# Four of eight query tiles on float16 parts, and one bfloat16 load where two float32 loads stood

## The chip, the cores and the metric

The kernel runs on one core of a Trainium2 chip. The metric is the device time of one launch, in microseconds (us); lower is better. The core has a matrix engine (TensorE, in the profile PE, with its weight loads as PEld), a vector engine (VectorE, DVE), a scalar engine (ScalarE, ACT), GpSimd (POOL) and SyncE (SP). DMA transfers are issued from queues, here almost all from those of SP and POOL. Operands lie in SBUF, 128 partitions wide; matrix products accumulate in eight PSUM banks.

## The reference

Two layers of a small diffusion transformer, on 256 tokens of x and 256 tokens of context, 2048 wide, in float32. Layer 0 is a Fourier branch, layer 1 an attention branch with a sink:

```python
def _fourier_branch(h, w_in, w_mix):
    u, z = jnp.split(h @ w_in, 2, axis=-1)
    f = jnp.fft.fft2(ug, axes=(1, 3), norm='ortho').real        # ug: u in 16 groups of 256
    f = jnp.einsum('bngc,gcd->bngd', f, w_mix)
    return f * jax.nn.silu(z)

# layer 1, x tokens (the context gives keys and values alone):
q, k, v, z = jnp.split(h @ w_in, [D_BRANCH, D_BRANCH + kvw, D_BRANCH + 2 * kvw], axis=-1)
q, k = _axial_rope(q, rows, cols), _axial_rope(k, rows, cols)
o = softmax over [scores of a band of 128 and of the context, sink]
y = o * jax.nn.silu(z)

# around each layer:
h = _rmsnorm(x, norm_g[i]) * (1 + scale) + shift                 # shift, scale, gate from c @ ada_w
x = x + gate * (y @ w_out[i])
```

Query, key and value come out of one weight matrix; the 4096 query columns are cut into eight tiles of 512 (eight heads of 64 each).

## The kernel before

**Precision.** A float32 product is made of three matmuls (`mm3`, lines 145 to 147): each operand is cut into a high and a low part, and high by high, high by low and low by high are summed in PSUM. There are two kinds of parts. `half_split` makes two float32r tiles of 128x1024: a cast on ACT (L66, `wh`) and a subtraction on DVE (L67, `wl`). `split16` makes one tile with two float16 halves (`wf`): a scaled copy on ACT (L137) and a multiply-and-subtract on DVE (L138); it needs a power of two `up` that brings the weights into float16's range, which is worked out from the sum of the squares of the weights. A pair of float32r tiles takes two of the six slots of the pool `ws`, a float16 pair one.

**Stages**, with their place in the profiled span:

1. 0 to 365 us: the Fourier branch's u part.
2. 365 to 658: the gate product z of layer 0, in blocks of 48 matmuls, on float16 parts; its weights `wz` come on SP's queue, 1 MiB a block, and are squared on ACT (L81) for their own scale. Beside it the adaptation products run on DVE (L792, `zr` and `wa` from `in_adw`), and the weights of later float16 products are read ahead, only to be squared and summed: `scan_loads` issues from POOL (L836) two loads of 128x512 float32 per step, `scan_sums` squares each on ACT (L829) with a running sum into a column of `scn`.
3. 658 to 996: the out product of layer 0 in two sweeps of 16 steps, float16; the same kind of reading ahead for the key and value weights and part of layer 1's out weights (`scan_loads1`, L821).
4. 996 to 1085: keys and values, float16. The normalised input of layer 1 is made as float16 pairs `hz` (16 tiles, both token groups) and, in `make_hx1`, for the x tokens as float32r parts `hx1`.
5. 1085 to 1543: attention. An order of units is written out by hand: query tile n+1 (eight units of 12 matmuls of 128x512) and four blocks of layer 1's gate z1 (two units of 24 matmuls of 128x256 each) stand beside the four attention blocks of tile n. All q and z1 units here are float32r: the weights are cut by `half_split` one unit ahead (`prep`), and the stationary operand of q is `hx1`. An attention block makes scores (L1499), the mask and row maximum on DVE (L1502), the exponential on ACT (L1506), the normalised probabilities on DVE (L1522) and ACT (L1521), a transposing DMA, and the product with v (L1533). `finish_q` makes the row scales and the rotary positions of a query tile.
6. 1543 to 1735: the out product of layer 1 and the last norm.

What sets the order is the program as written, with `issue_after` edges, and a scheduler that lays each engine's instructions in one queue. Weights stand in three raw tiles of 1 MiB, and the activations, the tiles read ahead among them, in a pool of 33 slots of 2 KB per partition.

Of the kernel before, what the change touches and what calls it, by code (L numbers as in the profile page):

```python
# [17 lines left out]
P = 128  # L18
# [4 lines left out]
N = 256  # L23
# [9 lines left out]
def tile_dit(ctx: ExitStack, tc: tile.TileContext, a: dict, out: bass.AP):  # L33
# [776 lines left out]
    ek, upk, dnk, kw = (keepc[:, c : c + 1] for c in range(4))  # L810
    gsz, shz = adab[:, 0, 1], adab[:, 0, 2]
    yq = adab[:, 1, 0].rearrange("p k s -> p (k s)")
    wst = [a["wkv"][i] for i in range(8)] + [a["wo1b"][i] for i in range(12)] + [a["wo1c"][i] for i in range(6)]
    scans1 = iter(range(52))

    def scan_loads1(n):
        for j in [next(scans1) for _ in range(n)]:
            for q in range(2):
                t = act()
                c = (j % 2 * 2 + q) * 512  # L820
                nc.gpsimd.dma_start(t, wst[j // 2][:, c : c + 512])  # L821
                c = j * 2 + q
                c += 80 if c < 28 else -28
                pend.append((t, scn[:, c : c + 1]))

    def scan_sums():
        while pend:
# [2 lines left out]

    def scan_loads(n):
        for j in [next(scans) for _ in range(n)]:
            for q in range(2):
                t = act()
                c = (j % 2 * 2 + q) * 512
                nc.gpsimd.dma_start(t, a["wo0"][j // 32, j % 32 // 2][:, c : c + 512])  # L836
                c = j * 2 + q - 64 * (j >= 40)
                pend.append((t, scn[:, c : c + 1]))

    def keep(dst, src):  # L840
        V.tensor_copy(dst, src)
        return dst

    def half_sum(sw):
        return [col_sum(scn[:, sw * 16 : sw * 16 + 64])] + [col_sum(scn[:, 80:108])] * (sw == 0)

    def half_scale(sw, sums_):
        x, up = sum_scale(sums_[0])
# [10 lines left out]
    with tc.tile_pool(name="yp", reuse_waits="tile", bufs=32) as ypool:  # L859
# [39 lines left out]
        if True:  # L899
# [104 lines left out]
        hbd = dram.tile([P, 2], F32, name="hbd")  # L1004
        hb1 = []

        def h1_bound():
            m, c = h_bound(gs1, sh1, False), tiny(F32, 4, "t4")
            V.tensor_copy(c[:, 0:1], m)
            for i, q in ((2, slice(80, 108)), (3, slice(0, 4))):  # L1010
                V.tensor_reduce(c[:, i : i + 1], scn[:, q], axis=AX.X, op=ALU.add)
            V.tensor_tensor(c[:, 1:2], c[:, 2:3], c[:, 3:4], op=ALU.add)
            nc.gpsimd.dma_start(hbd, c[:, 0:2])
            hb1.append(act())
            nc.gpsimd.dma_start(hb1[0][:, 0:N], hbd.rearrange("(o p) c -> o (p c)", o=1).broadcast_to([P, N]))

        def h1_scale():
            v = hb1[0][:, 0:N].rearrange("p (n c) -> p c n", c=2)
# [7 lines left out]
            V.tensor_reduce(s, v[:, 1], axis=AX.X, op=ALU.add)  # L1026
            V.tensor_scalar(kw, s, 2.0**-70, None, op0=ALU.max)
            V.tensor_scalar(kw.bitcast(I32), kw.bitcast(I32), 24, 23, op0=ALU.logical_shift_right, op1=ALU.logical_shift_left)
            V.tensor_scalar(upk.bitcast(I32), kw.bitcast(I32), -1.0, 204.0 * 2**23, op0=ALU.mult, op1=ALU.add)
            V.tensor_scalar(dnk.bitcast(I32), kw.bitcast(I32), ek.bitcast(I32), 2.0**23, op0=ALU.add, op1=ALU.max)  # L1030
        for i in range(32):
            sw, kg = i // 16, i % 16
            if kg == 0:
# [44 lines left out]
                    evac0(sw * 8 + b, o[b])  # L1078


    V.tensor_reduce(yq[:, 16:17], scn[:, 4:22], axis=AX.X, op=ALU.add)
    x1d = dram.tile([2, P, D], F32, name="x1d")
    gated = dram.tile([1, D], F32, name="gated")

# [34 lines left out]
    lay0.close()  # L1119

    l1c = ctx.enter_context(tc.tile_pool(name="l1c", reuse_waits="tile", bufs=1))
    rope = cload("rope", [P, 2, 2, 64], pool=l1c)
    mask = cload("mask", [P, 2, 512], pool=l1c)
    sink = cload("sink", [P, 64], pool=l1c)
# [14 lines left out]

    with tc.tile_pool(name="h1", reuse_waits="tile", bufs=16) as h1p:  # L1140
        hx1 = []
        v01, vs = [], []
        dsc = h1p.tile([P, 8], F32, name="dsc", bufs=1)
        ksc = h1p.tile([P, 6], F32, name="ksc", bufs=1)
# [2 lines left out]
        S.copy(ident16, ident)  # L1147
        kT = []
        with tc.tile_pool(name="kvp", reuse_waits="tile", bufs=2) as kvp:
            hz, ends = [], []  # L1150
            oner = kvp.tile([P, P], F32R, name="oner", bufs=1)
            S.activation(oner, ident, AF.Identity, bias=1.0, scale=0.0)
            ropek = act()[:, 0:N].rearrange("p (a b c) -> p a b c", a=2, b=2)
            for k in range(KT):
                z2 = kvp.tile([P, 1024], F16, tag="hz", name="hz", bufs=16)
                t = kvp.tile([P, 512], F32, tag="ht", name="ht")
                for s in range(2):
                    q = slice(s * N, (s + 1) * N)
                    h, l = (z2[:, s * 512 + c : s * 512 + c + N] for c in (0, N))
# [40 lines left out]
            for kg in range(8):  # L1200
# [11 lines left out]
                with tc.issue_after(last_cast[0]), tc.issue_after(last_sub[0]), tc.issue_after(ends[15][0]), tc.issue_after(ends[15][1]):  # L1212
                    for k in range(kg * 3 - 3, min(kg * 3, KT)) if kg else ():
                        make_hx1(k)
                    if kg == 7:
                        V.tensor_scalar(ropek, rope, dnk, None, op0=ALU.mult)
                for j in range(2):
                    k = kg * 2 + j
                    wh, wl = w[j]
                    for tb in range(4):  # L1220
                        c = tb // 2 * 512 + tb % 2 * P
                        for kv in range(2):
                            q = slice(kv * 512, (kv + 1) * 512)
                            mm3(o[tb][kv], hz[k][:, c : c + P], hz[k][:, N + c : N + c + P], wh[:, q], wl[:, q], k == 0, k == KT - 1)
            kr = []
            for tb in range(4):
                t, ab = act(), act(F32R)
# [43 lines left out]
        with tc.tile_pool(name="at", reuse_waits="tile", bufs=2) as at:  # L1271
# [88 lines left out]
            def finish_q(hk, oq):  # L1360
                sq = at.tile([P, 2, 4], F32, tag="sq", name="sq")
                for tb in range(2):
                    S.activation(act(), oq[tb], AF.Square, accum_out=sq[:, tb, 0:1])
                x, up, sc = (sq[:, :, c] for c in (1, 2, 3))
                qr = [act(), act()]
                roped(qr[0], oq[0], 0, actp, "act")
# [3 lines left out]
                roped(qr[1], oq[1], 1, actp, "act")  # L1370
# [46 lines left out]
            def prep(u):  # L1417
# [11 lines left out]
            def emit_unit():  # L1429
# [17 lines left out]
                if kind == "q":  # L1447
# [379 lines left out]
```

## Time and profile before

| what | value |
| --- | --- |
| time, median of 3 runs | 1736.21 us (1735.73 to 1736.79) |
| the profiled execution | 1736.42 us, of which the span is 1734.6 us |
| busy share of the span | PE 98%, DVE 79%, ACT 64%, POOL 16% |
| granted TensorE clock, mean | 0.998 |
| read from HBM, written | 419.30 MB, 12.59 MB |

The span is what the profiler saw between the first and the last instruction; 1.8 us lie around it. Busy time is not speed: consecutive matmuls overlap, so the time that one takes from the queue is the distance from its start to the next one's start, its pitch, and not its own busy time. A window is a stretch of the span, given as start and end in us.

### The profile page before, as it was taken

The numbers are of one execution on the slowest core, as the hardware profiler recorded it, in microseconds if no ns is written. First come the engines' busy times: TensorE is split into PE (matmuls) and PEld (weight loads), VectorE is DVE, ScalarE is ACT, GpSimd is POOL, SyncE is SP. The second block draws the span as 40 slices with busy tenths as digits, with TensorE's granted clock in tenths as the row PEclk, the third lists the DMA queues.
The fourth block names the chain that finished last, engine by engine and source line by source line (L and its number), as shares of the span: only waits on it lengthen the run. The fifth ranks groups of instructions, "written<-read, shape, count | busy, mean of one in ns | idle before, by whom it ended". The sixth has DMA issues, their size and how long they took to land. (4 is left out here: it accounts for less than half of the span.)

```text
span 1734.6 us, 28325 instructions
## 1 busy us (share of the span) xinstructions
PE 1703.1 (98%) x10379; PEld 1129.7 (65%) x10379; DVE 1373.2 (79%) x2390; ACT 1103.8 (64%) x2111; POOL 276.0 (16%) x429
## 2 busy tenths in 40 slices
PE   6999999999999999999999999999999999999997
PEld 4679999644444444446444654788888888876464
DVE  5779888798676787778689686888898989887755
ACT  5545555477777765464435397777787778777643
POOL 0001111211221204301420121300000000050001
PEclk9999999999999999999999999999999999999999
DMA  9998999869898968985997497489989899988643
GB/s 393 417 362 257 273 272 268 308 246 330 323 305 306 324 243 331 395 302 221 363 358 277 149 341 253 146 198 224 258 229 212 235 237 236 227 220 290 218 170 121
DMA packets 249195, 469.94 MB, mean 271 GB/s; under 512 B 171392, under 2 KB 171792, under 8 KB 222176
## 3 DMA queue, kind: packets, MB, share of 16 engines
q1 hardware_dynamic: 197568, 335.60, 59.3%
q0 software_dynamic: 47344, 125.58, 22.7%
q10 hardware_dynamic: 4144, 6.95, 1.2%
q8 instruction: 81, 1.33, 0.3%
q14 instruction: 58, 0.48, 0.1%
HBM read 419.30 MB, written 12.59 MB: 249 GB/s over the span
## 5 line engine op out<-in xcount | busy, mean ns | idle before, releaser
L67 DVE TENSOR_TENSOR wl<-raw,wh 128x1024 fp32r<-128x1024 f32 x152 | 188.4, 1256 | 43.1 <-ACT wh L66 33.0
L146 PE MATMUL ps<-act,wf 128*128 128x512 f16 x512 | 194.0, 379 | 0.0
L66 ACT CAST wh<-raw 128x1024 fp32r<-128x1024 f32 x152 | 157.3, 1046 | 57.6 <-PE ps L146 38.2
L147 PE MATMUL ps<-act,wf 128*128 128x512 f16 x512 | 191.1, 379 | 0.0
L145 PE MATMUL ps<-act,wf 128*128 128x512 f16 x512 | 189.8, 379 | 0.6 <-ACT wf L137 0.2
L145 PE MATMUL ps<-y,wf 128*128 128x512 f16 x448 | 169.8, 379 | 0.8 <-ACT wf L137 0.8
L146 PE MATMUL ps<-y,wf 128*128 128x512 f16 x448 | 169.8, 379 | 0.0
L145 PEld LDWEIGHTS <-wf 128*128 128x128 f16 x960 | 93.7, 98 | 113.4 <-ACT wf L137 4.2
L147 PEld LDWEIGHTS <-wf 128*128 128x128 f16 x960 | 93.9, 98 | 113.1
L147 PE MATMUL ps<-y,wf 128*128 128x512 f16 x448 | 164.9, 379 | 0.0
L146 PEld LDWEIGHTS <-wf 128*128 128x128 f16 x960 | 93.9, 98 | 109.0
L137 ACT ACTIVATE wf<-raw,nrm 128x1024 f16<-128x1024 f32 x56 | 63.5, 1145 | 131.4 <-PE ps L147 74.5
L145 PE MATMUL ps<-h,wh 128*128 128x256 f32 x512 | 144.4, 282 | 0.0
L146 PE MATMUL ps<-h,wh 128*128 128x256 f32 x512 | 142.7, 279 | 0.0
L147 PE MATMUL ps<-h,wl 128*128 128x256 f32 x512 | 142.6, 279 | 0.0
L1506 ACT ACTIVATE p<-ps,mx 128x512 f32<-128x512 f32 x128 | 87.8, 687 | 67.1 <-DVE mx L1502 64.7
L138 DVE SCALAR_TENSOR_TENSOR wf<-raw,tn,wf 128x1024 f16<-128x1024 f32 x64 | 79.8, 1282 | 42.6 <-ACT wf L137 42.6
L829 ACT ACTIVATE act<-act 128x512 f32<-128x512 f32 x178 | 109.4, 616 | 5.7 <-DMA act<-in_wo 4.4
L146 PE MATMUL ps<-wl,h 128*128 128x512 f32 x256 | 101.4, 396 | 0.0
L147 PE MATMUL ps<-wh,h 128*128 128x512 f32 x256 | 101.2, 395 | 0.0
L145 PEld LDWEIGHTS ps<-h,wh 128*128 128x128 f32 x512 | 96.1, 188 | 7.1 <-issue 5.5
L145 PE MATMUL ps<-wh,h 128*128 128x512 f32 x256 | 100.0, 402 | 0.0
(430 smaller groups left out, 4645.0 us busy)
## 6 DMA issues: line engine op xcount, KB each, us to landing
raw<-in_wz SPq DMA_DIRECT2D x64, 1024.0 KB, 6.3
raw<-in_awp SPq DMA_DIRECT2D x32, 1024.0 KB, 12.7
zr<-in_adw SPq DMA_DIRECT2D x64, 512.0 KB, 6.7
wa<-in_adw POOLq DMA_DIRECT2D x64, 512.0 KB, 6.3
act<-in_wo POOLq DMA_DIRECT2D x128, 256.0 KB, 7.4
raw<-in_wo SPq DMA_DIRECT2D x32, 1024.0 KB, 8.2
raw<-in_wq SPq DMA_DIRECT2D x32, 1024.0 KB, 5.8
raw<-in_wu SPq DMA_DIRECT2D x32, 1016.0 KB, 7.1
```

Source lines behind the costliest of these rows:

```text
L66: last_cast[0] = S.copy(h, src).ins
L67: last_sub[0] = eng.tensor_tensor(l, src, h.bitcast(F32), op=ALU.subtract).ins
L137: last_cast[0] = S.activation(w[:, 0], src, AF.Copy, scale=up).ins
L138: last_sub[0] = V.scalar_tensor_tensor(w[:, 1], src, up, w[:, 0], op0=ALU.mult, op1=ALU.subtract).ins
L145: PE.matmul(o, wh, xh, start=start, stop=False)
L146: PE.matmul(o, wh, xl, start=False, stop=False)
L147: return PE.matmul(o, wl, xh, start=False, stop=stop).ins
L829: S.activation(t, t, AF.Square, accum_out=c)
L1506: S.activation(pt[hh, tb], so[hh, tb], AF.Exp, bias=mx[:, hh, tb : tb + 1], scale=-1.0, accum_out=sm[:, hh, tb : tb + 1])
```

## The change

Query tiles 4 to 7 go over to float16 parts. Their weights are cut by `split16` with a scale `upq`, and the stationary operand is the x half of the float16 pairs that the key and value stage has made anyway: this half now lies in eight tiles `hzx` from the activation pool, two k each, and stays until tile 7 has used it; the context half stays in the key and value stage's own pool. `hx1` is still made, for z1 and tiles 0 to 3. 384 of the 768 matmuls of q change type.

For `upq` the squares of these weights are needed: `scan_loadsq` reads 32 half tiles of 512 KB (`sn<-in_wq`) during the gate product, one per block for blocks 4 to 27 and two for the last four. With that, every tile read ahead is one load of 128x1024, cast to bfloat16 by the DMA, and one Square on ACT, in place of two float32 loads of 128x512 and two Squares. The 178 loads of 256 KB become 89 of 512 KB, and 32 are new. In the key and value stage a second scale is worked out (one reduction and four small operations on DVE, `two_scales`) and a second table of positions is made (`ropeq`, one operation), which take the factor out again in `finish_q`; the Square there has a scale read from SBUF for tiles 4 to 7.

```diff
+    scansq = iter(range(32))
+    qsn = c32.rearrange("p k c -> p (k c)")[:, 0:32]
+    def scan_load(src, j, col):
+        t = actp.tile([P, 1024], BF16, tag="act", name="sn")
+        c = j % 2 * 1024
+        nc.gpsimd.dma_start(t, src[:, c : c + 1024])
+        pend.append((t, col))
+    def scan_loadsq(n):
+        for j in [next(scansq) for _ in range(n)]:
+            scan_load(a["wq"][4 + j // 8, j // 2 % 4], j, qsn[:, j : j + 1])
     def scan_loads(n):
         for j in [next(scans) for _ in range(n)]:
-            for q in range(2):
-                t = act()
-                c = (j % 2 * 2 + q) * 512
-                nc.gpsimd.dma_start(t, a["wo0"][j // 32, j % 32 // 2][:, c : c + 512])
-                c = j * 2 + q - 64 * (j >= 40)
-                pend.append((t, scn[:, c : c + 1]))
+            scan_load(a["wo0"][j // 32, j % 32 // 2], j, scn[:, j : j + 1])
...
                 scan_loads((2 if b % 3 else 1) if b < 28 else 0)
+                scan_loadsq(1 if b < 28 else 2)
...
+        def two_scales(v, up, dn):
+            V.tensor_reduce(kw, v, axis=AX.X, op=ALU.add)
...
             for k in range(KT):
-                z2 = kvp.tile([P, 1024], F16, tag="hz", name="hz", bufs=16)
+                if k % 2 == 0:
+                    zx.append(actp.tile([P, 1024], F16, tag="act", name="hzx"))
+                z2 = zx[k // 2][:, k % 2 * 512 : k % 2 * 512 + 512], kvp.tile([P, 512], F16, tag="hz", name="hz", bufs=16)
...
                     if kg == 7:
                         V.tensor_scalar(ropek, rope, dnk, None, op0=ALU.mult)
+                        V.tensor_scalar(ropeq, rope, dnq, None, op0=ALU.mult)
...
-                    S.activation(act(), oq[tb], AF.Square, accum_out=sq[:, tb, 0:1])
+                    S.activation(act(), oq[tb], AF.Square, scale=dnq if hk >= 4 else 1.0, accum_out=sq[:, tb, 0:1])
...
-                return half_split(raws1[src], i % 2)
+                return split16(raws1[src], i % 2, upq) if kind == "q" and n >= 4 else half_split(raws1[src], i % 2)
...
-                            pe_last[0] = mm3(o[tb], hx1[k][:, tb * P : (tb + 1) * P], hx1[k][:, N + tb * P : N + (tb + 1) * P], wh[:, q], wl[:, q], k == 0, k == KT - 1)
+                            t = hz[k][0] if n >= 4 else hx1[k]
+                            pe_last[0] = mm3(o[tb], t[:, tb * P : (tb + 1) * P], t[:, N + tb * P : N + (tb + 1) * P], wh[:, q], wl[:, q], k == 0, k == KT - 1)
```

POOL's queue at the start of the gate product, before (`wa` are adaptation weights, `act<-in_wo` the tiles read ahead):

```order
L790 DMA wa<-in_adw 128x1024
L836 DMA act<-in_wo 128x512 x4
L790 DMA wa<-in_adw 128x1024
L836 DMA act<-in_wo 128x512 x2
L790 DMA wa<-in_adw 128x1024
L836 DMA act<-in_wo 128x512 x4
L790 DMA wa<-in_adw 128x1024
```

The same place with the change (`sn` are the bfloat16 tiles):

```order
L790 DMA wa<-in_adw 128x1024
L821 DMA sn<-in_wo 128x1024 x2
L821 DMA sn<-in_wq 128x1024
L790 DMA wa<-in_adw 128x1024
L821 DMA sn<-in_wo 128x1024
L821 DMA sn<-in_wq 128x1024
L790 DMA wa<-in_adw 128x1024
```

Between two adaptation loads there stand two or three issues in place of two or four, and one of them is new in each block.

DVE's queue in attention beside query tile 4, before (L1502 is the mask and maximum, with its read of the accumulator in a row of its own, L1522 the normalising, L1470 and L1482 finish a block of z1):

```order
L1522 SCALAR_TENSOR_TENSOR f<-p,sm,f 128x512 x4
L67 TENSOR_TENSOR wl<-raw,wh 128x1024
L1470 SCALAR_TENSOR_TENSOR th<-th,ps 128x256
L67 TENSOR_TENSOR wl<-raw,wh 128x1024
L1482 SCALAR_TENSOR_TENSOR act<-ps,dsc,th 128x256
L1502 ISA ps,mx<-ps,mask,nsink,sq 128x512
L1502 ISA mx 128x1
L1502 ISA ps,mx<-ps,mask,nsink,sq 128x512
L1502 ISA mx 128x1
L1502 ISA ps,mx<-ps,mask,nsink,sq 128x512
```

The same place with the change (L1536, L1484, L1496 and L1516 are the former L1522, L1470, L1482 and L1502):

```order
L1536 SCALAR_TENSOR_TENSOR f<-p,sm,f 128x512 x4
L138 SCALAR_TENSOR_TENSOR wf<-raw,adab,wf 128x1024
L1484 SCALAR_TENSOR_TENSOR th<-th,ps 128x256
L138 SCALAR_TENSOR_TENSOR wf<-raw,adab,wf 128x1024
L1496 SCALAR_TENSOR_TENSOR act<-ps,dsc,th 128x256
L138 SCALAR_TENSOR_TENSOR wf<-raw,adab,wf 128x1024
L1516 ISA ps,mx<-ps,mask,nsink,sq 128x512
L1516 ISA mx 128x1
L1516 ISA ps,mx<-ps,mask,nsink,sq 128x512
L1516 ISA mx 128x1
L138 SCALAR_TENSOR_TENSOR wf<-raw,adab,wf 128x1024
L1516 ISA ps,mx<-ps,mask,nsink,sq 128x512
```

The cut of the query weights is the float16 one, it stands one to two units further ahead, and one of its operations now lies among the four mask operations of a block. On PE the order of the units is the same.

More of the change, by code (lines that the diff above doesn't have):

```diff
@@ L809, in tile_dit @@
     keepc = adab[:, 0, 0].rearrange("p k s -> p (k s)")
-    ek, upk, dnk, kw = (keepc[:, c : c + 1] for c in range(4))
+    ek, upk, dnk, kw, upq, dnq = (keepc[:, c : c + 1] for c in range(6))
     gsz, shz = adab[:, 0, 1], adab[:, 0, 2]
@@ L814, in tile_dit @@
     scans1 = iter(range(52))
+    scansq = iter(range(32))
[8 more added lines that the diff above has]
+            scan_load(a["wq"][4 + j // 8, j // 2 % 4], j, qsn[:, j : j + 1])
     def scan_loads1(n):
         for j in [next(scans1) for _ in range(n)]:
-            for q in range(2):
-                t = act()
-                c = (j % 2 * 2 + q) * 512
-                nc.gpsimd.dma_start(t, wst[j // 2][:, c : c + 512])
-                c = j * 2 + q
-                c += 80 if c < 28 else -28
-                pend.append((t, scn[:, c : c + 1]))
+            c = j + 64
+            scan_load(wst[j // 2], j, scn[:, c : c + 1])
     def scan_sums():
@@ L832, in scan_loads @@
         for j in [next(scans) for _ in range(n)]:
[L833 to L836, printed above, removed]
-                c = j * 2 + q - 64 * (j >= 40)
-                pend.append((t, scn[:, c : c + 1]))
+            scan_load(a["wo0"][j // 32, j % 32 // 2], j, scn[:, j : j + 1])
     def keep(dst, src):
@@ L844, in half_sum @@
     def half_sum(sw):
-        return [col_sum(scn[:, sw * 16 : sw * 16 + 64])] + [col_sum(scn[:, 80:108])] * (sw == 0)
+        return [col_sum(scn[:, sw * 32 : sw * 32 + 32])] + [col_sum(scn[:, 80:108])] * (sw == 0)
     def half_scale(sw, sums_):
@@ L1003, in tile_dit @@
         w_rate = {10: 1, 11: 1, 14: 2, 15: 2, 16: 2, 17: 1, 18: 1, 20: 1, 22: 2, 24: 3, 26: 3, 27: 3, 28: 3}
-        hbd = dram.tile([P, 2], F32, name="hbd")
+        hbd = dram.tile([P, 3], F32, name="hbd")
         hb1 = []
@@ L1009, in h1_bound @@
             V.tensor_copy(c[:, 0:1], m)
[L1010 to L1013, printed above, removed]
+            V.tensor_reduce(c[:, 1:2], scn[:, 64:80], axis=AX.X, op=ALU.add)
+            V.tensor_reduce(c[:, 2:3], qsn, axis=AX.X, op=ALU.add)
+            nc.gpsimd.dma_start(hbd, c[:, 0:3])
             hb1.append(act())
-            nc.gpsimd.dma_start(hb1[0][:, 0:N], hbd.rearrange("(o p) c -> o (p c)", o=1).broadcast_to([P, N]))
+            nc.gpsimd.dma_start(hb1[0][:, 0 : 3 * P], hbd.rearrange("(o p) c -> o (p c)", o=1).broadcast_to([P, 3 * P]))
+        def two_scales(v, up, dn):
+            V.tensor_reduce(kw, v, axis=AX.X, op=ALU.add)
+            V.tensor_scalar(kw, kw, 2.0**-70, None, op0=ALU.max)
+            V.tensor_scalar(kw.bitcast(I32), kw.bitcast(I32), 24, 23, op0=ALU.logical_shift_right, op1=ALU.logical_shift_left)
+            V.tensor_scalar(up.bitcast(I32), kw.bitcast(I32), -1.0, 204.0 * 2**23, op0=ALU.mult, op1=ALU.add)
+            V.tensor_scalar(dn.bitcast(I32), kw.bitcast(I32), ek.bitcast(I32), 2.0**23, op0=ALU.add, op1=ALU.max)
         def h1_scale():
-            v = hb1[0][:, 0:N].rearrange("p (n c) -> p c n", c=2)
+            v = hb1[0][:, 0 : 3 * P].rearrange("p (n c) -> p c n", c=3)
             s = tiny()
@@ L1025, in h1_scale @@
                 V.tensor_scalar(d, t, up, None, op0=ALU.mult)
[L1026 to L1030, printed above, removed]
+            two_scales(v[:, 1], upk, dnk)
         for i in range(32):
@@ L1078, in tile_dit @@
                     evac0(sw * 8 + b, o[b])
-    V.tensor_reduce(yq[:, 16:17], scn[:, 4:22], axis=AX.X, op=ALU.add)
+    V.tensor_reduce(yq[:, 16:17], scn[:, 80:89], axis=AX.X, op=ALU.add)
     x1d = dram.tile([2, P, D], F32, name="x1d")
@@ L1121, in tile_dit @@
     l1c = ctx.enter_context(tc.tile_pool(name="l1c", reuse_waits="tile", bufs=1))
+    ropeq = l1c.tile([P, 2, 2, 64], F32, name="ropeq")
     rope = cload("rope", [P, 2, 2, 64], pool=l1c)
@@ L1141, in tile_dit @@
         hx1 = []
+        hz, zx = [], []
         v01, vs = [], []
@@ L1149, in tile_dit @@
         with tc.tile_pool(name="kvp", reuse_waits="tile", bufs=2) as kvp:
-            hz, ends = [], []
+            ends = []
             oner = kvp.tile([P, P], F32R, name="oner", bufs=1)
@@ L1158, in tile_dit @@
                     q = slice(s * N, (s + 1) * N)
-                    h, l = (z2[:, s * 512 + c : s * 512 + c + N] for c in (0, N))
+                    h, l = (z2[s][:, c : c + N] for c in (0, N))
                     V.scalar_tensor_tensor(t[:, q], x1[k][:, q], gsz[:, k, s : s + 1], r_bc1[:, q] if k else r_ps[s], op0=ALU.mult, op1=ALU.mult)
@@ L1214, in tile_dit @@
                         make_hx1(k)
+                    if kg == 4:
+                        two_scales(hb1[0][:, 0 : 3 * P].rearrange("p (n c) -> p c n", c=3)[:, 2], upq, dnq)
                     if kg == 7:
                         V.tensor_scalar(ropek, rope, dnk, None, op0=ALU.mult)
+                        V.tensor_scalar(ropeq, rope, dnq, None, op0=ALU.mult)
                 for j in range(2):
@@ L1220, in tile_dit @@
                     for tb in range(4):
-                        c = tb // 2 * 512 + tb % 2 * P
+                        zt, c = hz[k][tb // 2], tb % 2 * P
                         for kv in range(2):
                             q = slice(kv * 512, (kv + 1) * 512)
-                            mm3(o[tb][kv], hz[k][:, c : c + P], hz[k][:, N + c : N + c + P], wh[:, q], wl[:, q], k == 0, k == KT - 1)
+                            mm3(o[tb][kv], zt[:, c : c + P], zt[:, N + c : N + c + P], wh[:, q], wl[:, q], k == 0, k == KT - 1)
             kr = []
@@ L1362, in finish_q @@
                 for tb in range(2):
-                    S.activation(act(), oq[tb], AF.Square, accum_out=sq[:, tb, 0:1])
+                    S.activation(act(), oq[tb], AF.Square, scale=dnq if hk >= 4 else 1.0, accum_out=sq[:, tb, 0:1])
                 x, up, sc = (sq[:, :, c] for c in (1, 2, 3))
                 qr = [act(), act()]
-                roped(qr[0], oq[0], 0, actp, "act")
+                tab = ropeq if hk >= 4 else rope
+                roped(qr[0], oq[0], 0, actp, "act", tab=tab)
                 V.tensor_scalar(x, sq[:, :, 0], 2.0**-70, None, op0=ALU.max)
@@ L1369, in finish_q @@
                 V.tensor_scalar(up.bitcast(I32), x.bitcast(I32), -1.0, 204.0 * 2**23, op0=ALU.mult, op1=ALU.add)
-                roped(qr[1], oq[1], 1, actp, "act")
+                roped(qr[1], oq[1], 1, actp, "act", tab=tab)
                 V.tensor_scalar(sc.bitcast(I32), x.bitcast(I32), kx.bitcast(I32), -30.0 * 2**23 - 2.0**31, op0=ALU.add, op1=ALU.add)
```

## The prediction, made before the change was run

> **What bounds the kernel now.** I read the page's shares first, then windows by stage, then the matmuls in order of time, to see whether the share of TensorE is real.
>
> ```profile
> PE 1703.1 (98%) x10379; PEld 1129.7 (65%) x10379; DVE 1373.2 (79%) x2390; ACT 1103.8 (64%) x2111; POOL 276.0 (16%) x429
> 364.89:616.24 251.35, 251.35 (x1208) 114.52 (x1207) 194.02 (x337) 189.74 (x408) 55.16 (x104) 1.00 0.89 318
> 825.82:970.70 144.88, 144.88 (x673) 65.70 (x673) 117.64 (x181) 62.81 (x121) 35.10 (x66) 1.00 0.87 318
> 996.00:1085.00 89.00, 88.87 (x436) 43.41 (x436) 65.72 (x130) 74.84 (x140) 15.81 (x29) 1.00 0.82 290
> 1282.60:1339.60 57.00, 57.00 (x434) 47.46 (x433) 50.67 (x95) 44.33 (x89) 1.69 (x3) 1.00 0.87 226
> 1339.60:1396.60 57.00, 57.00 (x434) 47.46 (x433) 50.65 (x95) 44.33 (x89) 2.95 (x3) 1.00 0.93 234
> 1453.60:1510.60 57.00, 57.00 (x434) 47.46 (x433) 50.66 (x96) 43.05 (x86) 0.94 (x1) 1.00 0.94 230
> ```
>
> A row of windows gives the stretch, its length, then busy us and instructions of PE, PEld, DVE, ACT and POOL, the granted clock, the share of the DMA engines and GB/s. The first is blocks 4 to 27 of the gate product, the second is of the out product of layer 0, the third keys and values, the others three of the four periods of attention beside which query tiles 4 to 7 are made. In each, PE is busy for all or nearly all of the window at full clock; in attention a period repeats at 57.0 us, with DVE at 50.66 of it, the nearest second. So here a matmul that takes less of the queue shortens the kernel, as long as DVE, ACT and the transfers keep up.
>
> What a matmul takes is its pitch:
>
> ```profile
> 1048.70 0.38 PE L146 MATMUL ps<-wf,hz 128*128 128x512 f16 x1
> ...
> 1055.82 0.38 PE L146 MATMUL ps<-wf,hz 128*128 128x512 f16 x1
> ```
>
> ```profile
> 1225.56 0.40 PE L145 MATMUL ps<-wh,h 128*128 128x512 f32 x1
> ...
> 1230.93 0.39 PE L147 MATMUL ps<-wh,h 128*128 128x512 f32 x1
> ...
> 1290.75 0.39 PE L147 MATMUL ps<-wh,h 128*128 128x512 f32 x1
> 1291.07 1.50 PE L1533 MATMUL ps<-ft,v 128*64 128x256 f16 x24
> ```
>
> The float16 rows are 33 steps of keys and values, without a break: 7.12 / 33 = 215.8 ns. The float32r rows are 23 steps of one query tile (two units): 5.37 / 23 = 233.5 ns. That this is the work and not a wait shows in that every step is alike. The last pair is the change of type: from a float32r query matmul to the float16 product with v it is 320 ns instead of 233.
>
> **The change, part by part.**
>
> *The matmuls of tiles 4 to 7.* 384 matmuls of 128x512 go from 233.5 to 215.8 ns: 384 x 17.7 ns = 6.8 us. The boundaries shift too: about 14 of these tiles' borders on the float16 products of attention (scores, v) no longer change type, at some 0.09 us each (320 less 233), 1.2 us; in return about five changes from float16 to float32r z1 are new, 0.4 us. Together -7.6 us, if PE finds its operands ready each time. All of it lies on the path, since PE has no pause in these periods.
>
> *Their weight cuts.* In these four periods a unit's cut goes from L66 and L67 to L137 and L138.
>
> ```profile
> L67 DVE TENSOR_TENSOR wl<-raw,wh 128x1024 fp32r<-128x1024 f32 x64 | 76.8, 1220 | 9.5 <-ACT wh L66 9.2 <-PE ps L146 0.3
> L66 ACT CAST wh<-raw 128x1024 fp32r<-128x1024 f32 x64 | 66.1, 1045 | 11.8 <-PE ps L146 11.8
> L138 DVE SCALAR_TENSOR_TENSOR wf<-raw,tn,wf 128x1024 f16<-128x1024 f32 x49 | 61.0, 1281 | 35.9 <-ACT wf L137 35.8
> L137 ACT ACTIVATE wf<-raw,tn 128x1024 f16<-128x1024 f32 x48 | 52.4, 1139 | 3.9 <-DVE tn L118 2.8 <-DVE tn L119 1.0
> ```
>
> The first two are groups of 1282.6 to 1510.6 (count, busy us, mean ns, idle time before), the others of the gate product. Eight cuts a period: DVE 8 x 61 ns = +0.5 us, ACT 8 x 94 ns = +0.8 us. DVE would then be at 51.2 of a period of 57.0 - 7.6 / 4 = 55.1 us, ACT at 45.1. The room of DVE must hold its own waits:
>
> ```profile
> DVE sm L1509 <- ACT es L1508: 14.5, 12, 1.2
> DVE wl L67 <- ACT wh L66: 9.2, 15, 1.0
> ACT wh L66 <- PE ps L146: 11.8, 12, 1.7
> ```
>
> These are totals over the four periods, how often, and the longest. The first is 3.6 us a period, a round trip through ACT in the row sums that stays: 51.2 + 3.6 = 54.8, below 55.1 by 0.3 us. The others are waits that come from a lack of slots (a float32r pair takes two of six, and ACT waits for PE to give them back) and can shrink, since a float16 pair takes one. In the order of DVE the cuts stand further ahead, so a cut is less likely to be late; but one of them now stands among the mask operations, and 1.28 us there is put before an exponential (L1506). It just fits; I take off 0.5 us for cuts or masks late by a little, which gives **-7.1 us**, and the bounds are -8.5 (boundaries worth twice as much) and -4.5 (a third of the gain waits for DVE).
>
> *Finishing a tile.* The Square with a scale from SBUF, two per tile, has its nearest rows in L66 against L137, which differ by 94 ns as fixed against read scale: +0.2 us per period on ACT, with 10 us spare. `ropeq` and the second scale in keys and values are six small operations on DVE, none as large as the 1024 columns of L67 (1.2 us), so under 7 us, and DVE has 23 us spare in the third row above (89 - 65.7). Without that cover they would cost that once.
>
> *The scans.* In the gate product 1.67 steps a block (two in two blocks of three) were four or two loads and Squares, and become one load and one Square each, plus one new.
>
> ```profile
> L829 ACT ACTIVATE act<-act 128x512 f32<-128x512 f32 x78 | 48.0, 616 | 0.0
> L829 ACT ACTIVATION_READ_ACCUMULATOR act<-act 128x1 f32 x78 | 14.7, 188 | 0.0
> L81 ACT ACTIVATE sq<-raw 128x1024 bf16<-128x1024 f32 x48 | 50.0, 1046 | 0.0
> L903 ACT ACTIVATE act<-ps,tn 128x512 f32<-128x512 f32 x27 | 18.2, 686 | 54.8 <-PE ps L147 54.8
> L836 POOL DMA_DIRECT2D act<-in_wo x80 | 42.5, 538 | 4.6 <-DMA cb<-in_crow 2.2 <-ACT wf L137 0.9 <-ACT act L903 0.9
> ```
>
> ACT per block: 3.33 x (616 + 188) = 2.7 us becomes 2.67 x (1046 + 188) = 3.3 us, +0.6 us where a block is 251.35 / 24 = 10.5 us and ACT used 7.9. ACT waits 54.8 us for PE in the window, so the 15 us more are covered. A Square that reads bfloat16 has no row; 1046 ns stands for it, since two of the old ones, 2 x 616, come near it. POOL issues 64 loads in place of 80 here; no load that casts is in this trace, so the cost of one issue lies between a plain one, 538 ns, and an accumulating one,
>
> ```profile
> L208 POOL DMA_DIRECT2D raw<-in_wu x13 | 19.3, 1488 | 114.8 <-DVE wm L199 92.6 <-DMA pz<-in_wz 22.3
> raw<-in_wu POOLq DMA_DIRECT2D x13, 508.0 KB, 7.5
> wa<-in_adw POOLq DMA_DIRECT2D x64, 512.0 KB, 6.3
> act<-in_wo POOLq DMA_DIRECT2D x128, 256.0 KB, 7.4
> ```
>
> so 34 to 95 us of POOL for 43 before, in 251 us of which POOL used 55: nothing either way, though what waits behind the issues is `wa` for DVE's adaptation products.
>
> *What the scans move.* This is the part that can hurt. 24 blocks x 0.524 MB = 12.6 MB are added to 318 GB/s x 251.35 us = 79.9 MB: 92.5 MB, 368 GB/s if the time stays. At the window's own share, 0.89 x 251.35 / 79.9 = 2.80 us of all engines per MB, that needs 259 us: 7.7 us too long. But the share falls with the sort of traffic:
>
> ```profile
> 50.00:100.00 50.00, 46.94 (x364) 31.66 (x360) 32.92 (x78) 22.88 (x40) 0.00 (x0) 1.00 1.02 417
> 700.00:750.00 50.00, 50.00 (x233) 22.67 (x232) 40.79 (x60) 24.57 (x47) 13.90 (x26) 1.00 0.98 378
> ```
>
> Here 417 and 378 GB/s moved, the second beside a PE that never paused; at 2.45 us per MB (1.02 x 50 us for 20.9 MB) the stage needs 227 us. The tiles also become half as large in SBUF while the bytes read stay. And a late transfer first eats a distance:
>
> ```profile
> 488.16 0.33 SPq L50 DMA_DIRECT2D raw<-in_wz x1
> ...
> 515.70 2.18 ACT L137 ACTIVATE wf<-raw,tn 128x1024 f16<-128x1024 f32 x2
> ...
> raw<-in_wz SPq DMA_DIRECT2D x64, 1024.0 KB, 6.3
> ```
>
> The block's weights are issued at 488.16, land some 6.3 us later, and are cut from 515.70: 21 us to spare. I take nothing, with +7.7 us as the upper bound for plain loads, and more if a cast is dear (below).
>
> The Trainium skill speaks against this part: "DMA: Bandwidth & Descriptors", section "Specifications", puts the share of HBM of one core at about 358 GB/s. By it the stage would last 92.5 MB / 358 GB/s = 258 us as an estimate, 7 us more, and the change would come out even. This trace does not agree with it as a bound: 417 GB/s in the window above.
>
> *Sum.* -7.1 + 0 + 0 = -7.1 us on the profiled 1736.42 us (1734.6 span and 1.8 around it): 1729.3. The median of the runs is 0.2 us below the profiled one, so I say 1729.2.
>
> **Rivals.**
>
> *A. DVE becomes the bound in attention.* 0.3 us of room per period is thin; if the waits for the cuts, 2.3 us per period (9.2 / 4), stay beside the 3.6, DVE needs 51.2 + 5.9 = 57.1, no less than today. Half of that staying gives about 56.0 per period, so the gain is 4 x 1.0: about 1732.5. For it: DVE is the second engine in every period. Against it: the slots are doubled for just these cuts, and the wait L67 on L66 is partly idle time in which nothing was due.
>
> *B. The gate product becomes bound by transfers (the side of slower).* Its mechanism is one: `wz` and the scans share the 16 engines, and from above 251.35 / 92.5 = 2.72 us per MB the weights fall behind. At 2.80 the stage takes 259 us: 1729.2 + 7.7 = 1737. If a load that casts takes as much longer as an accumulating one (7.5 against 6.3 us, 1.19 times), the 33.5 MB of scans (21.0 before, 12.6 new) cost 33.5 x 2.80 x 0.19 = 18 us more: 1755. Between them, 1741 is where I put it. For it: share 0.89 already, and 0.89 x 92.5 / 79.9 = 1.03 is no less than the highest share that a window above shows. Against it: PE kept its pace at 0.98, and the 21 us of distance would have to go first.
>
> *C. The adaptation loads and products fall out of step with the cuts of layer 0's out product.*
>
> ```profile
> ACT wf L137 <- DVE acc L792: 38.1, 8, 9.9
> 863.47 1.28 DVE L138 SCALAR_TENSOR_TENSOR wf<-raw,nrm,wf 128x1024 f16<-128x1024 f32 x1 [4.46 <-ACT wf L137]
> ...
> 866.12 1.22 DVE L792 CUSTOM_DVE_ANT_0 wa<-wa,cb 128x1024 f32<-128x1024 f32 x1
> 867.26 0.38 PE L145 MATMUL ps<-y,wf 128*128 128x512 f16 x1
> ```
>
> The wait is of 825.82 to 970.70: ACT's copies already stand behind these products. The cut at 863.47 ends at 864.75, 2.5 us before PE's first matmul on it. Four or five products of 1.22 us put before a cut make it 3 us late, twice of which takes 6 us: about 1735. That the order of these stages moves little speaks against it.
>
> *D. The change doesn't do what it says:* float16 matmuls with stationary `hzx` would not reach 215.8 beside the scores. Then nothing is gained, 1736. The third stage, with the same operands, speaks against it.
>
> **How the numbers follow.** Forecast 0.62, A 0.12, B 0.14, C 0.08, D 0.02, others 0.02. The forecast's own range is 1727.7 to 1732. 0.2% of 1736 is 3.5 us, about what a measurement of this kernel can tell from no change; faster is then below 1732.7, slower above 1739.7. Faster gets the forecast and a good third of A, 0.66; slower gets the upper half of B and a bit of others, 0.12; the rest, 0.22, is within. The range reaches from 1727.5, near the forecast's full gain, up over A, C, D and the plain price of B: 1738.5. What is left out is mostly B with dear casts.
>
> **What would show it.** Right: rows `ps<-wf,hzx` at 216 ns pitch in attention; the four periods at 55 to 55.4 us; the gate product at 10.5 us a block with a share of DMA near 0.95 or above, and no pause of PE before its L145. Wrong: periods of 56 us or more with PE waiting for `wf` of L138 or the scores' PSUM (A); `PE ps L145 <- ACT wf L137` or `ACT wf <- DMA raw<-in_wz` with tens of us in the gate product, or landing times of `raw<-in_wz` over 10 us (B); such waits from 830 to 970 with `DVE acc L792` behind them (C). If a scan issue takes over 3 us on POOL, or half tiles arrive so late that ACT waits for them in front of the weight cuts, the whole view of the gate product falls.

## The result, and the profile after

The changed kernel takes 1757.41 us (median, 1755.04 to 1760.43), the kernel before 1735.99 us beside it: a ratio of 1.0124 with a 95% interval of 1.0106 to 1.0141. It is slower by 21 us where 7 us less were forecast, and lies outside the range of 1727.5 to 1738.5. The profiled execution is the fastest of the four, 1755.04 us with a span of 1753.3, 18.7 us more than before.

Where these 18.7 us lie can be read by setting the starts of the 10379 matmuls, which stand in the same order in both traces, against each other. The lag is 0.2 us when the gate product begins and 0.2 us when it ends; the first sweep of layer 0's out product adds 15.3 us, the second 11.7, keys and values 0.4, and attention takes 9.0 back: 0.2 + 15.3 + 0.1 + 11.7 + 0.4 - 9.0 = 18.7.

The windows of the profile after, with the same columns as before (length, then busy us of PE, PEld, DVE, ACT and POOL, granted clock, DMA share, GB/s): the gate product, the two stretches of the out product with the pauses, and a period of attention.

```profile
364.89:616.24 251.35, 251.35 (x1209) 114.47 (x1208) 194.13 (x337) 207.85 (x376) 47.25 (x89) 1.00 0.99 301
713.00:760.00 47.00, 37.67 (x149) 15.57 (x147) 40.08 (x60) 13.87 (x21) 4.36 (x9) 0.85 0.76 270
880.00:930.00 50.00, 40.38 (x179) 17.70 (x178) 40.16 (x64) 13.24 (x15) 5.31 (x10) 0.90 0.86 285
1365.46:1420.22 54.76, 54.76 (x434) 38.47 (x433) 51.04 (x93) 44.85 (x88) 2.47 (x2) 1.00 1.01 239
```

The gate product holds its pace with the share of the transfer engines at 0.99. A period of attention is 54.76 us, 2.25 less than the 57.01 before, four times over. The query matmuls have the pitch that was forecast; in order of time, of tile 5:

```profile
1366.75 0.38 PE L147 MATMUL ps<-wf,hzx 128*128 128x512 f16 x1
...
1371.28 0.38 PE L147 MATMUL ps<-wf,hzx 128*128 128x512 f16 x1
```

These are 21 steps, 4.53 / 21 = 215.7 ns. So attention does what the change is for, and the loss is in the out product of layer 0, which the diff touches only in how it reads ahead. There PE stands still:

```profile
882.62 0.38 PE L147 MATMUL ps<-y,wf 128*128 128x512 f16 x1
892.38 0.61 PE L145 MATMUL ps<-y,wf 128*128 128x512 f16 x1 [9.38 <-ACT wf L137]
```

PE waits for a weight cut by ACT; ACT and DVE wait in turn. The waits of 840 to 930 (waiting line, released by, total us, times, longest):

```profile
ACT wf L137 <- DVE acc L792: 45.0, 4, 26.6
...
DVE junk L792 <- DMA wa<-in_adw: 23.1, 1, 23.1
```

and the two instructions on DVE between which those 23 us lie:

```profile
864.21 1.28 DVE L138 SCALAR_TENSOR_TENSOR wf<-raw,nrm,wf 128x1024 f16<-128x1024 f32 x1
888.64 1.23 DVE L792 CUSTOM_DVE_ANT_0 junk<-wa,cb 128x1024 f32<-128x1024 f32 x1 [23.14 <-DMA wa<-in_adw]
```

An adaptation product needs a load `wa` that has not landed. `wa` takes a slot of the pool `ws`, which the weight cuts use too, and DVE works in order, so the cuts stop. Before, the same load was just in time: it landed at 864.8 us, and its product began then, without a wait:

```profile
864.85 1.22 DVE L792 CUSTOM_DVE_ANT_0 junk<-wa,cb 128x1024 f32<-128x1024 f32 x1
```

The load is late because of what stands ahead of it on POOL. POOL's issues in the second sweep, first of the profile before:

```profile
825.12 1.06 POOL L790 DMA_DIRECT2D wa<-in_adw  x2 [23.13 <-DVE gt L1046]
826.17 3.19 POOL L821 DMA_DIRECT2D act<-in_wkv  x6
830.66 0.54 POOL L821 DMA_DIRECT2D act<-in_wkv  x1 [1.30 <-DMA wa<-in_adw]
...
855.09 0.53 POOL L790 DMA_DIRECT2D wa<-in_adw  x1 [0.78 <-DMA act<-in_wkv]
...
861.26 0.53 POOL L790 DMA_DIRECT2D wa<-in_adw  x1
```

then of the profile after:

```profile
840.61 1.06 POOL L790 DMA_DIRECT2D wa<-in_adw  x2 [27.89 <-DVE gt L1051]
841.66 3.19 POOL L821 DMA_DIRECT2D sn<-in_wkv  x6
845.60 0.54 POOL L821 DMA_DIRECT2D sn<-in_wkv  x1 [0.76 <-DMA wa<-in_adw]
...
860.44 0.53 POOL L821 DMA_DIRECT2D sn<-in_wo1b  x1 [2.06 <-DMA sn<-in_wkv]
863.83 0.53 POOL L821 DMA_DIRECT2D sn<-in_wo1b  x1 [2.86 <-DMA sn<-in_wkv]
...
879.11 0.53 POOL L790 DMA_DIRECT2D wa<-in_adw  x1 [0.72 <-DMA sn<-in_wo1b]
```

Two things are to be seen. The first: in both traces eight loads go out one behind the other (two `wa`, six scans), and the ninth issue waits for the landing of the first. From there on each issue starts behind the landing of the eighth load before it, nearly always 0.3 to 0.6 us behind, and idles up to 4 us for it. Whether the chip or the program sets the eight, no run here shows. The second: before, 22 scan loads of 256 KB stand in front of the next `wa`, and it goes out 30 us behind the first pair (825.12 to 855.09). After, 19 loads stand there, but of 512 KB, and it goes out 38.5 us behind (840.61 to 879.11), while PE uses up its cut weights. In the first sweep 21 loads stand in front of a `wa` in both kernels, and the same doubling of their bytes puts its issue 33 us behind the one before it instead of 21. So the loads in front are about as many as before, and nearly twice the bytes. The late `wa` itself is no slower: it lands 9.5 us after its issue, before 9.7. No byte of the query weights is read in the second sweep.

### The profile page after: what moved, and what is told of

Its sections match the earlier page's. It is cut to its first block, busy times and chain, and to the rows that moved or that the text cites. A ratio compares the mean times of both kernels' runs of the same rounds, so it can differ in the third digit from the quotient of the medians.

```text
span 1753.3 us, 28081 instructions
## 1 busy us (share of the span) xinstructions
PE 1702.5 (97%) x10379; PEld 1095.3 (62%) x10379; DVE 1376.5 (79%) x2395; ACT 1125.1 (64%) x1997; POOL 248.2 (14%) x372
## 5 line engine op out<-in xcount | busy, mean ns | idle before, releaser
L67 DVE TENSOR_TENSOR wl<-raw,wh 128x1024 fp32r<-128x1024 f32 x120 | 150.8, 1266 | 50.9 <-ACT wh L66 29.1
L145 PE MATMUL ps<-y,wf 128*128 128x512 f16 x448 | 172.6, 386 | 10.2 <-ACT wf L137 10.2
L147 PE MATMUL ps<-y,wf 128*128 128x512 f16 x448 | 170.3, 384 | 9.6 <-DVE wf L138 9.6
L146 PE MATMUL ps<-y,wf 128*128 128x512 f16 x448 | 172.9, 386 | 0.0
L66 ACT CAST wh<-raw 128x1024 fp32r<-128x1024 f32 x120 | 124.3, 1045 | 59.2 <-PE ps L146 33.5
L138 DVE SCALAR_TENSOR_TENSOR wf<-raw,adab,wf 128x1024 f16<-128x1024 f32 x82 | 112.2, 1380 | 30.3 <-ACT wf L137 30.2
L836 ACT ACTIVATE sn<-sn 128x1024 bf16<-128x1024 bf16 x121 | 126.3, 1044 | 11.7 <-DMA sn<-in_wq 6.9
L137 ACT ACTIVATE wf<-raw,adab 128x1024 f16<-128x1024 f32 x82 | 91.9, 1142 | 40.4 <-PE ps L147 16.3
L792 DVE CUSTOM_DVE_ANT_0 junk<-wa,cb 128x1024 f32<-128x1024 f32 x48 | 58.6, 1221 | 51.2 <-DMA wa<-in_adw 51.0
```

The lines of the kernel that those rows point to most:

```text
L66: last_cast[0] = S.copy(h, src).ins
L67: last_sub[0] = eng.tensor_tensor(l, src, h.bitcast(F32), op=ALU.subtract).ins
L137: last_cast[0] = S.activation(w[:, 0], src, AF.Copy, scale=up).ins
L138: last_sub[0] = V.scalar_tensor_tensor(w[:, 1], src, up, w[:, 0], op0=ALU.mult, op1=ALU.subtract).ins
L145: PE.matmul(o, wh, xh, start=start, stop=False)
L146: PE.matmul(o, wh, xl, start=False, stop=False)
```

## The experiments

Three theories were set against each other. **Q (queue):** a half tile read ahead takes one slot of the pool of 33 where two stood, so twice the bytes run ahead in POOL's queue, in front of `wa`. **B (bytes):** the 16.8 MB of query weights are too much for the transfers. **K (cast):** a load that casts costs more per byte read. For comparison over all runs, the wait of the adaptation products (L792) for `wa` between 660 us and the end of the out product is 11.4 us before and 49.3 us after.

### No reading of the query weights

```diff
-                scan_loadsq(1 if b < 28 else 2)
...
         def h1_bound():
+            V.memset(qsn, 0.5)
```

> The changed kernel without the 32 loads and Squares of the query weights; the scale of tiles 4 to 7 comes from a constant in place of their sum. Theory Q (queue: a scan as one half-size tile takes one slot where two stood, so twice the bytes run ahead in POOL's queue, in front of the adaptation loads wa; DVE waits for wa in order and the weight cuts behind it come late): the second sweep of layer 0's out product keeps its pause of about 10 us, the first keeps some, 1740 to 1757 us. Theory B (bytes: the 16.8 MB more are what the stage cannot carry): no pause is left, 1735.99 - 9.0 = 1727. Theory K (the cast makes a load slower per byte read): pauses stay, 1740 to 1757.

Measured: 1750.69 us, ratio 1.0078 (1.0063 to 1.0093). Attention gains 9.0 us, and 0.8 more are gained behind it; the pauses stay, with 11.3 us lost in the first sweep and 11.4 in the second. 2.5 us are lost ahead of the gate product in this trace, which is of the slowest of the four runs; why is not known. B falls as the main cause: without one byte of the query weights the kernel is still slower than before.

### The packing of the scans alone

On the kernel before, only the form of the scans is changed:

```diff
-            for q in range(2):
-                t = act()
-                c = (j % 2 * 2 + q) * 512
-                nc.gpsimd.dma_start(t, a["wo0"][j // 32, j % 32 // 2][:, c : c + 512])
+            t = actp.tile([P, 1024], BF16, tag="act", name="sn")
+            nc.gpsimd.dma_start(t, a["wo0"][j // 32, j % 32 // 2][:, j % 2 * 1024 : j % 2 * 1024 + 1024])
```

> The kernel before, with its 178 scan loads of 128x512 float32 packed into 89 of 128x1024 cast to bfloat16 and one Square each; nothing read for the query weights, all of attention in float32r. Q: slower than before by 10 to 27 us, 1746 to 1763, with the same wait of DVE for wa. B: as before, 1736. K: slower, 1746 to 1763.

Measured: 1755.74 us, ratio 1.0109 (1.0092 to 1.0125), and the same wait in the second sweep:

```profile
871.00 0.53 POOL L790 DMA_DIRECT2D wa<-in_adw  x1 [0.73 <-DMA sn<-in_wo1b]
...
880.50 1.23 DVE L792 CUSTOM_DVE_ANT_0 junk<-wa,cb 128x1024 f32<-128x1024 f32 x1 [22.77 <-DMA wa<-in_adw]
```

This part of the change, with nothing of its purpose, costs 19 us: 7.5 in the first sweep and 11.4 in the second. The loss in the second sweep is the change's own within 0.3 us; that in the first is smaller than the change's 15.3. The last loads of the query weights go out only at 659 us in the change; the run without them loses 11.3 there, so they can stand for about half of the difference, and the other half was not explained.

### All bytes, without the cast, two slots for a half tile

The whole change, but each scan is two loads of 128x512 float32 again:

```diff
-        t = actp.tile([P, 1024], BF16, tag="act", name="sn")
-        c = j % 2 * 1024
-        nc.gpsimd.dma_start(t, src[:, c : c + 1024])
+        for q in range(2):
+            t = act()
+            c = (j % 2 * 2 + q) * 512
+            nc.gpsimd.dma_start(t, src[:, c : c + 512])
```

> The changed kernel with all scans, those of the query weights too, as two float32 loads of 128x512 and two Squares, as before: all the bytes, no cast, two slots a half tile. Q: the adaptation loads stand between the scans again; no long pause, 1727 to 1731. B: the first sweep, which takes the bytes that the gate product could not, keeps its 15 us: 1741. K: 1727 to 1731.

Measured: 1730.80 us (1729.88 to 1733.32), ratio 0.9966 (0.9953 to 0.9979). PE's lag against the kernel before stays at 0.46 us through the gate product and both sweeps. So the 16.8 MB more cost nothing in this order, and the gate product ran at 365 GB/s for it:

```profile
364.89:616.24 251.35, 251.35 (x1208) 114.47 (x1207) 189.89 (x333) 218.08 (x498) 80.71 (x152) 1.00 0.97 365
```

The first three query periods on float16 take 54.76 us, the last 56.58, where PE pauses once for 1.6 us, and 0.8 us more go just behind. That is why it gains 6 us and not 9.

### The cast with half-size loads

As the kernel just above, with `t = actp.tile([P, 512], BF16, ...)` in place of `t = act()`: the loads cast, a half tile still takes two slots, and the order on POOL is nearly the same.

> The changed kernel with every scan as two loads of 128x512 cast to bfloat16 and two Squares: the cast and all the bytes stay, a half tile takes two slots again. Q: 1727 to 1731, like the float32 scans. K: the pauses stay though the queue is in the old order, 1740 to 1757. B: 1741.

Measured: 1745.80 us with a wide spread (1739.27 to 1757.71), ratio 1.0053 (1.0034 to 1.0072). The trace is of the fastest of the ten runs; where the others lost more, no trace shows. In it neither account fits: no pause in the first sweep, three of 2.0 to 3.8 us in the second. Here K may have a part. POOL's queue (q0) in the gate product, with packets, MB written and share of the 16 engines, of the change, then of the float32 pairs, then of the half-size casts:

```profile
q0 software_dynamic: 12671, 30.41, 52.0%
```

```profile
q0 software_dynamic: 13695, 47.20, 51.4%
```

```profile
q0 software_dynamic: 21826, 30.37, 57.8%
```

The same bytes are read in all three (the count gives those written, half of them for a cast). The 128x1024 cast of the change costs the engines what a plain load costs, 52.0 against 51.4%; cut into halves it costs 57.8. So a half-size cast costs more per byte read, as K says, and the change's own does not. That this is what makes the pauses here is argued from the share, not shown.

### The change's loads, on two slots

The change as it is, but the Square of a scan writes to a second tile of the pool, so that a half tile takes two slots:

```diff
-        pend.append((t, col))
+        pend.append((t, actp.tile([P, 1024], BF16, tag="act", name="sq2"), col))
...
-            S.activation(t, t, AF.Square, accum_out=c)
+            S.activation(t2, t, AF.Square, accum_out=c)
```

> The changed kernel with one edit: the Square of a scan writes to a second tile of the pool in place of its own, so that a half tile takes two of the 33 slots again; the 121 loads of 128x1024 with cast and all the bytes stay. Q (queue: the run-ahead in front of wa): the pauses go, 1736.9 - 9.0 = 1728, up to 1731. K (a cast load costs more per byte read, as the half-size casts suggested): a pause of 5 to 10 us in the second sweep stays, 1737 to 1747.

Measured: 1738.78 us (1736.14 to 1745.04), ratio 1.0011 (1.0001 to 1.0021). In the out product the pauses are gone, as Q said: from 620 to 915 us, in the time of the kernel before, PE's lag does not move by 0.1 us, and L792 waits 21 us for `wa` in place of 49.3, about as long as in the kernel with float32 pairs, which has no pause (19.2). But 8 us go in the gate product, where the change lost nothing:

```profile
364.89:616.24 251.35, 246.43 (x1173) 110.89 (x1172) 185.45 (x323) 200.69 (x361) 46.58 (x88) 0.99 0.96 288
```

There the order on ACT has moved as well, and weight cuts come late behind Squares; what would set that right was not tried. The time lies where K put it, but without K's pause; Q has the place right and misses the number.

The same edit on the packed kernel without the query weights:

> The packed scans alone on the kernel before (nothing read for the query weights, attention in float32r), with a half tile on two slots. Q: as before, 1736 to 1739, where the same on one slot took 1755.7. K: 1743 to 1750.

Measured: 1739.56 us, ratio 1.0014 (1.0005 to 1.0023), where one slot took 1755.74. It differs from that kernel by the slots and the order that follows from them; 16 of its 19 us are undone, and the wait for `wa` falls from 46.8 to 20.7 us. The two runs do not restore the old order, though: between two `wa` of the out product there stand at most 6 and 4 loads of 512 KB, fewer bytes than the 21 and 22 loads of 256 KB of the kernel before. They show that the pauses go when the run-ahead goes, and not that each slot counts alike.

### The adaptation loads on another queue

```diff
-                                nc.gpsimd.dma_start(wf, a["adw"][i, kh, fg][:, q])
+                                nc.sync.dma_start(wf, a["adw"][i, kh, fg][:, q])
```

> The changed kernel with the adaptation loads wa issued from SP's queue in place of POOL's: the scans run ahead as in the change, but nothing stands behind them. Q: DVE no longer waits long for wa, 1728 to 1735. S (saturation: the scans that run ahead fill the transfer engines, so that any load lands late, whatever its queue): pauses of 10 us and more stay, 1745 to 1757.

Measured: 1772.60 us, ratio 1.0201 (1.0184 to 1.0218), slower than both values. But the loss has changed places. The gate product, which lasts until 701 us here, and then the second sweep:

```profile
365.00:700.00 335.00, 306.35 (x1402) 132.99 (x1401) 223.57 (x397) 233.05 (x418) 43.88 (x83) 0.96 0.90 259
868.00:958.00 90.00, 89.15 (x413) 40.34 (x412) 78.50 (x120) 35.40 (x46) 4.24 (x8) 1.00 0.93 309
```

43 us are lost in the gate product, where `wa` now stands in SP's queue beside the weights `wz`; from there to the end of the out product no pause is left. That agrees with Q: `wa` is no longer late when no scan stands in front of it in its queue. But theory S is not put to the same test, since the scans go out earlier than in the change: 12 of the 19 are out when the first `wa` of the second sweep goes, at 868.4 us, and the last goes at 872.9. What speaks against S is the trace of the change, where the late `wa` lands no later after its own issue than before (9.5 and 9.7 us). DVE's order moves with these edits too: in the change the late product of the second sweep stands one weight cut earlier than before. Here it stands two cuts earlier and does not pause PE, so that order alone is not the cause. For a better kernel the move is none.

### Packed in the gate product, pairs in the out product

```diff
+            if j < 40:
                 scan_load(a["wo0"][j // 32, j % 32 // 2], j, scn[:, j : j + 1])
+            else:
+                scan_pair(a["wo0"][j // 32, j % 32 // 2], j, j * 2 - 40)
```

with `scan_pair` the two float32 loads of before, also for the key, value and out weights of layer 1.

> The changed kernel with the scans of the gate product as in the change (one cast load of 128x1024, those of the query weights too) and those of the out product as two float32 loads of 128x512 each. Q: what lost time in the change was the run-ahead in the out product alone, since the gate product kept its pace there; so no pause is left, 1736.9 - 9.0 = 1728, up to 1731. K (a cast load is dear in itself): the gate product's cast loads leave too much to the out product, a pause of some us in its first sweep, 1732 to 1740.

Measured: 1730.51 us (1727.78 to 1731.58), ratio 0.9958 (0.9944 to 0.9971). The gate product with the packed loads is at the pace of before (the lag stays at -0.1 us), the first sweep loses 0.6 us, the second nothing, and the wait for `wa` is 14.1 us. The time is within Q's range and below K's. Two periods of attention take 55.7 in place of 54.76. It is the fastest kernel here beside the float32 pairs, from which its interval does not part it, and it beats both the kernel before and the change.

## Why the prediction was wrong

- **The matmuls of tiles 4 to 7: the pitch right, the borders not as read.** 215.7 ns were measured for 215.8. The sum for attention was -7.6 before a deduction of 0.5; it measured -9.0 us. Set against each other one by one over the four periods, the matmuls give it as follows. 360 query steps behind one another go from 233.3 to 215.8 ns, -6.3 us. The step behind the first query matmul after an attention product goes from 336 to 226 ns, eight times, -0.9. The way out to the product with v, which the prediction took for a change of type, hardly moves, 323 to 309 ns, eight times, -0.1. Even where both sides are float16 (1372.57 to 1372.88 in the profile after) the step is 310 ns. The new changes to float32r z1, put at +0.4 us, measure -0.05. And z1's own 753 steps, on which the sum had nothing, go from 118.4 to 116.1 ns, -1.7 us; why was not found. So the sum came near partly by chance: some of what it looked for at the borders lies elsewhere.
- **Weight cuts and DVE's room (rival A): A did not come.** Three periods of 54.76 us have 51.0 to 52.1 us of DVE in them; the sum said 51.2. The round trip that was to fill the rest shrank: the waits of the row sums for ACT (`sm`) are 5.0 us from 1290 to 1570, against 19.5 from 1260 to 1550 before. That the cuts further ahead give DVE other work there is the likely reason, argued from the order and not tried alone.
- **What the scans move (rival B): right in taking nothing.** About 92 MB were read in the gate product at share 0.99 without a late weight (as many as with the float32 pairs, 365 GB/s in 251 us). The estimate of 258 us by the Trainium skill's ~358 GB/s per core ("DMA: Bandwidth & Descriptors", "Specifications") did not come true either; those 365 GB/s were held without a loss.
- **The scans on POOL: the step that failed.** It counted each issue at 538 to 1488 ns and found "nothing either way", with `wa` behind the issues named and not followed. The price of an issue was right (544 ns for `sn<-in_wo`), but what passes between two issues is the landing of the eighth load before, for which POOL idles 1 to 4 us. And the prediction worked out the gate product alone, where the order alternates, and not the out product, where 21 and 19 scans of 512 KB stand in front of a `wa`, in place of 21 and 22 of 256 KB. So the term that was put at nothing measured 27 us: 15.3 in the first sweep and 11.7 in the second. The order could be read beforehand: the packing halves the slots that a half tile takes, and so the same number of loads ahead carries twice the bytes.
- **Rival C had the mechanism and not the size.** The adaptation loads did fall out of step with the cuts of the out product. But the case was priced by products of 1.22 us put ahead of a cut, twice 3 us of delay, and held at 0.08; it measured 27 us, since a product that waits for its load keeps DVE for up to 23 us and not for its own 1.22. Against it stood that the order of these stages moves little; that holds for the number of loads on POOL and nearly for DVE, but the bytes in front of `wa` nearly doubled.

## What to carry to other kernels

Packing a transfer into a smaller tile also changes how far it runs ahead: what a pool of slots held back before now goes into the same queue in front of other loads, and the load that someone waits for stands behind it. Read the order of each DMA queue for the loads that an in-order engine consumes, count the bytes in front of each and the time of their landing, not the number of loads and the time of their issue, and do so in every stage that the helper serves, not only where the edit stands. A side edit that "saves" can be tried alone: here the packing by itself cost 19 us, and the purpose of the change by itself was worth 6.

## What the hardware showed that was not expected

PE comes back slowly from a pause, which no rival of the prediction counted. After the 9.4 us without work at 882 us its matmuls take twice the pitch at first, at a granted clock of 0.62 in that stretch:

```profile
892.40:897.00 4.60, 4.60 (x14) 1.79 (x15) 4.60 (x8) 0.96 (x1) 1.06 (x2) 0.62 0.46 132
```

```profile
892.78 0.63 PE L146 MATMUL ps<-y,wf 128*128 128x512 f16 x1
893.20 0.63 PE L145 MATMUL ps<-y,wf 128*128 128x512 f16 x1
...
895.34 0.63 PE L146 MATMUL ps<-y,wf 128*128 128x512 f16 x1
...
896.26 0.38 PE L145 MATMUL ps<-y,wf 128*128 128x512 f16 x1
```

From 892.78 to 895.34 are 6 steps of 427 ns, about twice 215.7. From the first matmul, 892.38, to the first at full pitch, 895.76 to 896.04, the slow stretch is 3.4 us. The Trainium skill has this in "TensorE: Matmul & The Clock Gate", Part 1 (the clock gate): half the clock after an idle window, about 3.4 us of work until full clock, 426.7 ns cold for 512 columns. The trace agrees in the pitch; the 3.4 us hold for this stretch, but the two behind the pauses of the first sweep (4.0 and 6.1 us) lasted 6.0 and 5.5 us. The prediction priced a pause by its length alone. Over the two sweeps the pauses themselves are 19.6 us (4.0, 6.1, 9.8 and 0.6, less a pitch each) of the 27.0 us lost; of the rest, 7.4 us, the slow matmuls make 7.3: 14, 13 and 8 steps of about 425 ns in place of 215.7, 2.9 + 2.7 + 1.7 us. And a load that casts 128x1024 float32 to bfloat16 takes the transfer engines about as long as plain loads of the same bytes (52.0 against 51.4% of the gate product above), though it writes half: the smaller tile saves slots, not time on the engines.
